# Two products for each block in the even input projection, with both sums added by VectorE

## Chip, cores and metric

The kernel runs on one core of one Trainium2 chip. The metric is the device time of one execution in microseconds; of the kernel before there are three runs, and their median counts.

## The reference, cut to what matters

A trunk of two layers on 256 tokens with 2048 features. The first (even) layer begins with one projection `z`, which feeds a recurrence (part A, 16 heads of 64 features) and a gated linear recurrence (part B).

```
z = x @ ev_w_in                                   # 256 x 2048 times 2048 x 5408
# part A, columns 0 .. 3359: r, k, v and three low-rank pieces
z = z + (token_shift(z) - z) * mu                 # token_shift: one token back
r, k, v, w_lo, a_lo, g_lo = split_cols(z, A_SIZES)
kk = k * k_k;  kk = kk / max(sqrt(sum(kk * kk)), 1e-12)      # by head
...                                               # recurrence over the tokens, group norm, gate
# part B, columns 3360 .. 5407
xb, gate = split(z, 2)
xc = causal_dwconv(xb, conv_w, conv_b)            # 4 taps
...                                               # two gates from xc, a scan over the tokens
y_b = gelu(gate) * h
y = concatenate([y_a, y_b]) @ ev_w_out
```

Then come layer norm, a feed-forward part, a gated addition, and the second (odd) layer, which the change leaves as it is.

## The kernel before, in words

Features lie on the 128 partitions and the 256 tokens in the columns. Each weight and each activation is held as a high and a low part, and a product is the sum of high x high, high x low and low x high. The activations' parts lie side by side in one tile of 512 columns (`hls[k]`: high in columns 0 to 255, low in 256 to 511). `wchunk` (L110) loads half a row of weights (128 x 1024, SP's queue), and ScalarE (`hi`) and VectorE (`lo`) split it, in this layer in slices of 256 columns.

`mm3` (L134) has two forms. With `one`, a block of 128 features takes three matmuls of 256 columns into the first half of a PSUM bank (L138, L139, L140). Without it, the high weights take both parts in one matmul of 512 columns into the whole bank (L142) and the low weights the high part into its first half (L143); the two halves of the bank have then to be added, which `evac` (L186) does: ScalarE copies the second half to SBUF, VectorE adds the first. `gproj` (L145) runs a row of 16 blocks and yields 0.32 us (`BLOCK`) after each; it is a generator, so that a row can be taken piece by piece.

The even layer's input projection has 43 rows of weights (`evin`), all with `one=True`:

- 3 rows for the low-rank pieces (`lora`, L645), one after the other at the start;
- 3 rows for each of 8 pairs of heads (`stage1`, L657; "a head" below is such a pair): block(1) for the keys, block(0), block(2) for the values;
- 2 rows for each of 8 steps of part B (`rglru`, L919): one for the convolution, one for the gate.

`shifted` (L634) takes the rows of part A: ScalarE scales the sum in PSUM by 1 - mu (L638), VectorE adds the sum one token back, scaled by mu (L639). `rglru` reads its first row's PSUM in one ScalarE operation (L924) and three of VectorE (L927), and its second row's in a gelu (L959).

TensorE's order is the program's. `run` (L1027) takes the recurrence of a head (`stage2`, L751), whose steps yield about how long TensorE would wait, and fills each such time with pieces of `filler` (L1012): the next head's `stage1`, then `rglru`, and with the last head the first rows of the output projection. Two places of this order matter below.

- In `stage1`, block(1) is followed by the scaling and shift of `kr`, by `kk` and its square; eight blocks of block(0) are emitted, then the sum of the squares over a head's features (`group_pow`, L293), whose power POOL takes; later the result is spread out (L284).
- In `stage2`, two matmuls (L814) give B, which ScalarE copies; then a loop of 15 steps on VectorE, each a product and a sum, works on its columns and ends in Dt, which TensorE takes at L780. After each step two blocks of the filler are emitted.

ScalarE and VectorE instructions of `stage1` and `stage2` are emitted through `Ahead` (L49 in the profile), which lets them come before others that were emitted up to 20 and 60 instructions earlier; those of `shifted`, `evac` and `rglru` have no such right. All engines run in the order fixed when the program is built. Tiles of the tag `t` come from a ring of 11, PSUM banks of these rows from a ring of 3 (`pp`).

Of the kernel before, what the change touches and what calls it, by code (L numbers as in the profile page):

```python
# [30 lines left out]
def drain(g):  # L31
    """runs a generator to its end and returns what it returns"""
    while True:
        try:
            next(g)
        except StopIteration as e:
            return e.value


class Ahead:  # L40
    """an engine whose instructions come before those emitted up to n instructions earlier, where it has the choice"""
# [11 lines left out]
class Core:  # L53
# [21 lines left out]
    def load_const(self, n, after):  # L75
        """a table of constants, loaded once after is there: the loads that come first are short of bandwidth"""
        t = getattr(self, n)
        self.nc.scalar.copy(t[:, 0:1], after[:, 0:1])
        self.nc.sync.dma_start(t, self.a[n])
# [18 lines left out]
    def xt(self, m, name, dt=F32R, w=2 * S):  # L98
        """a tile for block m of 16, in one of two rings that hold 8 blocks and one more"""
        return self.xpool.tile([P, w], dt, tag="xa" if m < 8 else "xb", name=self.nm(name))  # L100

    def ps(self, tag=None):
        """a PSUM bank; without a tag, from all of them in turn"""
# [5 lines left out]
    # ---- weights: load, then split into the two parts that single-pass products carry  # L109
    def wchunk(self, src, keep=None):  # L110
        """high and low part of a piece of weights; keep: makes a tile that holds them for longer"""
# [16 lines left out]
    def hl_split(self, dst, src):  # L128
        """dst[:, :256] and dst[:, 256:] become the high and low part of src."""
# [4 lines left out]
    def mm3(self, ps, hi, lo, hl, first, last, one=False):  # L134
        """a block's products; they add up over both halves of ps, or, with one, in its first half alone"""
# [9 lines left out]
    def gproj(self, src, hls, group=8, one=False, more=None, parts=None):  # L145
        """src [128, KT*128] in DRAM, hls the KT activation tiles; returns PSUM [128, 512] whose halves add up
        (one: all in the first). more: (high, low, activations) of one further block, last in the sum;
        parts: src's pieces where they are on chip already. Yields the time of TensorE after each block"""
# [14 lines left out]
    def pieces(self, srcs, k0=0, group=8, soon=0):  # L163
        """the k-tiles k0 .. of several rows of weights, split by instructions that others wait for less"""
# [5 lines left out]
    def projs(self, srcs, ws, hls, group=8):  # L170
        """proj of several rows side by side, each activation tile serving all of them as soon as it is there;
        ws: the first pieces of the weights"""
# [13 lines left out]
    def evac(self, ps, out):  # L186
        """out = sum of the halves"""
# [5 lines left out]
    # ---- residual and layer norm, features on the partitions  # L193
# [6 lines left out]
    def ln_pre(self, m, hl):  # L200
        """s = alpha * x for one block of 128 features"""
# [5 lines left out]
    def ln_set(self, m, ps, hl):  # L207
        """s = alpha * x + y"""
# [7 lines left out]
    def ln_more(self, m, ps):  # L216
        """s += y, with y in the first half of ps"""
# [3 lines left out]
    def ln_stat(self, m):  # L221
        """the sums of s and s * s over the features grow; those of the last block stay apart"""
# [15 lines left out]
    def ln_end(self):  # L238
        """mean and 1 / deviation of each token, worked out with the tokens on the partitions"""
# [17 lines left out]
    def ln_apply(self, g, b):  # L257
        """the normed activations as high and low tiles"""
# [18 lines left out]
    def tok_bcast(self, src, w, b, tag=None):  # L277
        """src [token of a tile of 128, n] -> PSUM [n-th block of w partitions.., tokens], each value on its w partitions"""
# [8 lines left out]
    def group_pow(self, sq, w, scale, c, op, aux, tmp):  # L287
        """(scale * sum of sq over groups of w features, op, c) ** -0.5 [token, (half of the tokens, group)]"""
# [11 lines left out]
    def group_rsqrt(self, sq, w, scale, c, op, aux, tmp, tag):  # L300
        """group_pow in PSUM, on the group's partitions"""
# [53 lines left out]
    def ple_proj(self, l, phl, half, pool=None):  # L355
        """p Wp / 2 for eight blocks of 128 features: two to a tile of pool, or out to DRAM"""
# [20 lines left out]
    def ple_back(self, l, pool):  # L377
        """the blocks that ple_proj put into DRAM"""
# [7 lines left out]
    def ple(self, l, pool, emit):  # L386
        """x + sigmoid(x Wg) * (p Wp); emit(m, tile) takes the blocks of the result"""
# [7 lines left out]
        for m in range(KD):  # L395
            # x + (tanh(g / 2) + 1) * (p Wp / 2)
# [17 lines left out]
# ---- layout of the inputs  # L414
# [4 lines left out]
def col(v):  # L419
    """feature vector -> [128, n] with feature n*128 + p at [p, n]"""  # L420
    return v.reshape(-1, 128).T


def buckets():
    """bucket of each relative position 127 .. -255 (REL_BUCKETS 32, REL_MAX_DIST 128)"""
# [36 lines left out]
def odd_consts():  # L462
    """centring over the first 64 rows, twice; one-hot buckets"""
# [6 lines left out]
def tile_w(W):  # L470
    """[K, M] -> [M/128, 128, K]: block m holds, for each row p of each block of K, its 128 columns"""
# [4 lines left out]
def lay_out(I):  # L476
    """the inputs as the kernel reads them: moved, repeated or padded with zeros, never computed with"""
# [25 lines left out]
    # even layer  # L503
# [34 lines left out]
    # odd layer  # L538
# [22 lines left out]
# ---- even layer's mixer  # L561
# [9 lines left out]
# TensorE time to fill in between the steps of a recurrence, in us  # L571
# [7 lines left out]
def q(t, w=64):  # L579
    """[128, 4*w] -> [128, 4, w]"""  # L580
    return t.rearrange("p (c w) -> p c w", w=w)


class Even:
# [49 lines left out]
    def shifted(self, m, j, out, parts=None):  # L634
        """z * (1 - mu) + shift(z) * mu, z = block m of the input projection; j its place in mu"""
        nc, k = self.nc, self.k
        ps = yield from k.gproj(k.a["evin"][m], self.x, one=True, parts=parts)
        nc.scalar.mul(out, ps[:, 0:S], self.omu[:, j:j + 1])  # L638
        nc.vector.scalar_tensor_tensor(out[:, 1:], ps[:, 0:S - 1], k.v("mu", j), out[:, 1:], op0=ALU.mult, op1=ALU.add)  # L639
# [17 lines left out]
    def stage1(self, i):  # L657
        """projections of two heads and everything that goes feature by feature"""
# [10 lines left out]
        # decay and in-context rate  # L669
# [765 lines left out]
```

## Time and profile before

| | us |
|---|---|
| median of three runs | 2447.64 |
| the three runs | 2447.42, 2447.64, 2456.84 |
| span of the profiled execution | 2455.2 |
| the profiled execution's own time | not told apart; of the three runs only that of 2456.84 is longer than the span |

The span runs from the first to the last instruction. The time of an execution holds the span and a little around it. Busy shares are of the span. A row of TensorE's timeline shows a start and a modelled length; matmuls overlap, and so the distance from one start to the next is what one costs, not its length.

### The profile page before, as it was taken

How to read it: one execution, taken by the hardware profiler on the slowest of the kernel's cores; microseconds unless marked ns; L12 is line 12 of the kernel's file. 1: busy time of each engine (PE TensorE's matmuls, PEld its weight loads, DVE VectorE, ACT ScalarE, POOL GpSimd, SP SyncE). 2: the span in 40 equal slices, each digit the busy share in tenths (PEclk: the TensorE clock that was granted, in tenths of full speed). 3: DMA queues.
4: the chain of work that ended last, by engine and by line, in shares of the span. 5: the costliest groups of instructions: out<-in, count | busy, mean ns of one | idle time of the engine just before them, and what ended most of it. 6: DMA issues, size and time to landing. Idle time of an engine off the chain costs nothing.

```text
span 2455.2 us, 40424 instructions
## 1 busy us (share of the span) xinstructions
PE 2423.2 (99%) x15136; PEld 2161.8 (88%) x15136; DVE 1790.2 (73%) x3756; ACT 1386.7 (56%) x2612; POOL 88.0 (4%) x98
## 2 busy tenths in 40 slices
PE   8999999999999999999999999999999999999999
PEld 8999999888888888888888998888888888888888
DVE  7888888887777777655569697787777777555577
ACT  6767776456555555443346567465555555444454
POOL 0000000010000000000010030010000000000010
PEclk9999999999999999999999999999999999999999
DMA  7333333656666666666656654555555565566655
GB/s 241 118 123 121 105 116 114 185 176 201 191 190 189 189 190 189 184 188 188 187 172 199 190 155 130 190 181 188 188 186 184 188 187 184 180 188 189 188 170 174
DMA packets 128484, 429.38 MB, mean 175 GB/s; under 512 B 14096, under 2 KB 21920, under 8 KB 128288
## 3 DMA queue, kind: packets, MB, share of 16 engines
q1 hardware_dynamic: 128288, 426.80, 55.9%
q8 instruction: 119, 1.95, 0.3%
q14 instruction: 77, 0.63, 0.1%
HBM read 422.52 MB, written 4.22 MB: 174 GB/s over the span
## 4 chain that ended last, share of the span: by engine, by line
PE 89%; issue 5%; DVE 3%; ACT 2%; DMA 1%; POOL 0%; POOLq 0%; ACTq 0%; DVEq 0%; SPq 0%
PE a L142 27%; PE pp L142 18%; PE a L143 14%; PE pp L143 9%; PE pp L138 4%; PE pp L139 4%; PE pp L140 4%; PE a L780 2%; DVE lo L49 1%; PE a L138 1%; PE a L139 1%; PE a L140 1%; DMA raw<-evin 1%; PE a L814 0%; ACT hi L49 0%
## 5 line engine op out<-in xcount | busy, mean ns | idle before, releaser
L49 DVE TENSOR_TENSOR lo<-raw,hi 128x1024 fp32r<-128x1024 f32 (+4 forms) x1160 | 1008.9, 884 | 499.9 <-ACT hi L49 495.4
L49 ACT CAST hi<-raw 128x1024 fp32r<-128x1024 f32 (+4 forms) x1160 | 860.7, 768 | 792.0 <-PE a L142 325.4
L142 PE MATMUL a<-x,hi 128*128 128x512 f32 x2048 | 725.4, 397 | 9.0 <-DVE x L273 9.0
L143 PE MATMUL a<-x,lo 128*128 128x256 f32 x2048 | 572.0, 279 | 0.0
L142 PEld LDWEIGHTS a<-x,hi 128*128 128x128 f32 x2048 | 385.3, 188 | 102.9 <-DVE x L273 11.0
L142 PE MATMUL pp<-x,hi 128*128 128x512 f32 x1248 | 445.0, 397 | 3.6 <-DVE x L273 3.6
L143 PEld LDWEIGHTS a<-x,lo 128*128 128x128 f32 x2048 | 386.6, 189 | 0.4 <-DVE lo L49 0.2
L143 PE MATMUL pp<-x,lo 128*128 128x256 f32 x1248 | 348.5, 279 | 0.0
L142 PEld LDWEIGHTS pp<-x,hi 128*128 128x128 f32 x1248 | 234.9, 188 | 62.3 <-DVE x L273 6.3
L142 PE MATMUL a<-g,hi 128*128 128x512 f32 x792 | 277.7, 393 | 0.0
L138 PE MATMUL pp<-x,hi 128*128 128x256 f32 x800 | 248.3, 310 | 6.7 <-ACT x L131 6.7
L143 PEld LDWEIGHTS pp<-x,lo 128*128 128x128 f32 x1248 | 235.6, 189 | 0.1
L139 PE MATMUL pp<-x,hi 128*128 128x256 f32 x800 | 226.1, 283 | 0.7 <-DVE x L132 0.7
L140 PE MATMUL pp<-x,lo 128*128 128x256 f32 x800 | 226.7, 283 | 0.0
L143 PE MATMUL a<-g,lo 128*128 128x256 f32 x792 | 221.0, 279 | 0.0
L142 PE MATMUL pp<-g,hi 128*128 128x512 f32 x528 | 185.3, 393 | 0.0
L142 PEld LDWEIGHTS a<-g,hi 128*128 128x128 f32 x792 | 148.4, 187 | 35.3
L138 PEld LDWEIGHTS pp<-x,hi 128*128 128x128 f32 x800 | 152.4, 191 | 11.1 <-ACT x L131 6.7
L139 PEld LDWEIGHTS pp<-x,hi 128*128 128x128 f32 x800 | 152.7, 191 | 5.4 <-issue 3.6
L321 ACT ACTIVATE cv<-u,vec_sb 128x256 f32<-128x256 f32 x176 | 105.6, 600 | 88.1 <-DVE u L318 85.8
L140 PEld LDWEIGHTS pp<-x,lo 128*128 128x128 f32 x800 | 151.2, 189 | 0.2 <-issue 0.2
L143 PEld LDWEIGHTS a<-g,lo 128*128 128x128 f32 x792 | 148.4, 187 | 0.0
(415 smaller groups left out, 3407.8 us busy)
## 6 DMA issues: line engine op xcount, KB each, us to landing
raw<-up SPq DMA_DIRECT2D x352, 512.0 KB, 4.5
raw<-dn SPq DMA_DIRECT2D x160, 512.0 KB, 3.7
raw<-evin SPq DMA_DIRECT2D x86, 512.0 KB, 4.1
raw<-pg SPq DMA_DIRECT2D x64, 512.0 KB, 4.5
raw<-odout SPq DMA_DIRECT2D x32, 512.0 KB, 4.5
raw<-evout SPq DMA_DIRECT2D x16, 512.0 KB, 3.8
raw<-dn SPq DMA_DIRECT2D x32, 256.0 KB, 2.7
raw<-evout SPq DMA_DIRECT2D x16, 448.0 KB, 3.4
```

Source lines behind the costliest of these rows:

```text
L49: return getattr(self.eng, name)(*args, **kw)
L138: nc.tensor.matmul(ps[:, 0:S], hi, hl[:, 0:S], start=first, stop=False)
L139: nc.tensor.matmul(ps[:, 0:S], hi, hl[:, S:2 * S], start=False, stop=False)
L140: nc.tensor.matmul(ps[:, 0:S], lo, hl[:, 0:S], start=False, stop=last)
L142: nc.tensor.matmul(ps[:, 0:2 * S], hi, hl, start=first, stop=False)
L143: nc.tensor.matmul(ps[:, 0:S], lo, hl[:, 0:S], start=False, stop=last)
L321: nc.scalar.activation(y, u[:, 2:], AF.Identity, bias=self.v(f"cb{l}", j), scale=self.v(f"cw2{l}", j))
L780: T.matmul(ps[:, c * P:(c + 1) * P], lhs[:, c * P:(c + 1) * P], AR4[:, c] if rhs is AR else rhs[:, c * P:(c + 1) * P], start=True, stop=True)
```

## The change

The rows of the even input projection are computed in the second form of `mm3`: `one=True` is dropped from the three calls of `gproj`. Each row's two halves are added by `evac`, in `shifted` and for the convolution into a new tile `z` of the ring `t`, which the operations behind then read in the place of PSUM, and for the gate into `g`, on which the gelu then works in place. The loads, the order of the rows, the fill times and everything else stay. The diff also takes comments out; these parts are left out here.

```
     def shifted(self, m, j, out, parts=None):
         nc, k = self.nc, self.k
-        ps = yield from k.gproj(k.a["evin"][m], self.x, one=True, parts=parts)
-        nc.scalar.mul(out, ps[:, 0:S], self.omu[:, j:j + 1])
-        nc.vector.scalar_tensor_tensor(out[:, 1:], ps[:, 0:S - 1], k.v("mu", j), out[:, 1:], op0=ALU.mult, op1=ALU.add)
+        ps = yield from k.gproj(k.a["evin"][m], self.x, parts=parts)
+        z = k.t("z")
+        k.evac(ps, z)
+        nc.scalar.mul(out, z, self.omu[:, j:j + 1])
+        nc.vector.scalar_tensor_tensor(out[:, 1:], z[:, 0:S - 1], k.v("mu", j), out[:, 1:], op0=ALU.mult, op1=ALU.add)
...
     def rglru(self, j, yout):
-        ps = yield from k.gproj(k.a["evin"][27 + 2 * j], self.x, one=True)
+        ps = yield from k.gproj(k.a["evin"][27 + 2 * j], self.x)
+        z = k.t("z")
+        k.evac(ps, z)
         xc = self.r1("xc")
-        A.activation(xc, ps[:, 0:S], AF.Identity, bias=k.v("bconv_b", j), scale=k.v("bconv3", j))
+        A.activation(xc, z, AF.Identity, bias=k.v("bconv_b", j), scale=k.v("bconv3", j))
         for n in range(3):
             d = 3 - n
-            V.scalar_tensor_tensor(xc[:, d:], ps[:, 0:S - d], k.v(f"bconv{n}", j), xc[:, d:], op0=ALU.mult, op1=ALU.add)
+            V.scalar_tensor_tensor(xc[:, d:], z[:, 0:S - d], k.v(f"bconv{n}", j), xc[:, d:], op0=ALU.mult, op1=ALU.add)
...
-        rest = k.gproj(k.a["evin"][28 + 2 * j], self.x, one=True)
+        rest = k.gproj(k.a["evin"][28 + 2 * j], self.x)
...
         ps = yield from rest
         g = self.r1("g")
-        A.activation(g, ps[:, 0:S], AF.Gelu_apprx_tanh)
+        k.evac(ps, g)
+        A.activation(g, g, AF.Gelu_apprx_tanh)
```

## Rows read from the trace of the kernel before

**Rows 1.** The head of the page: the span, and each engine's busy time, share of the span and instructions.
```profile
span 2455.2 us, 40424 instructions
...
PE 2423.2 (99%) x15136; PEld 2161.8 (88%) x15136; DVE 1790.2 (73%) x3756; ACT 1386.7 (56%) x2612; POOL 88.0 (4%) x98
```

**Rows 2.** The table of stretches: the stretch in us from the span's start and its length, then each engine's busy time with its instructions, the granted clock of TensorE, the busy share of the DMA engines and GB/s. The last stretch lies in the feed-forward part of the even layer.
```profile
0.00:50.00 50.00, 42.26 (x320) 41.17 (x320) 37.58 (x112) 35.26 (x92) 3.59 (x10) 1.00 0.78 268
...
200.00:250.00 50.00, 49.81 (x391) 47.17 (x389) 42.59 (x141) 37.42 (x104) 2.35 (x2) 1.00 0.36 114
...
600.00:700.00 100.00, 100.00 (x578) 87.42 (x578) 72.59 (x127) 57.23 (x90) 0.00 (x0) 1.00 0.62 190
```

**Rows 3.** Waits of TensorE, of the stretches 0 to 50 us and 410 to 460 us: engine, operation and line, what it waited for, us in total, times, the longest.
```profile
PE a L293 <- ACT sq L49: 0.2, 1, 0.2
...
PE a L780 <- DVE Dt L49: 0.9, 1, 0.9
```

**Rows 4.** DMA issues of the whole program, those of the input projection's weights: queue, count, KB each, median us to landing.
```profile
raw<-evin SPq DMA_DIRECT2D x86, 512.0 KB, 4.1
```

**Rows 5.** Timeline of TensorE in two heads: start in us, length in us, engine, line, operation, and what is written and read. L293 of the keys, a block behind another matmul, undisturbed blocks, and the first matmul on Dt.
```profile
113.81 0.53 PE L293 MATMUL a<-cst_sb,sq 128*128 128x32 f32 x4
...
158.59 0.60 PE L835 MATMUL a<-cst_sb,ET 128*128 128x128 f32 x4
158.95 0.36 PE L138 MATMUL pp<-x,hi 128*128 128x256 f32 x1
...
159.38 0.28 PE L138 MATMUL pp<-x,hi 128*128 128x256 f32 x1
...
160.82 0.28 PE L138 MATMUL pp<-x,hi 128*128 128x256 f32 x1
...
162.07 0.53 PE L293 MATMUL a<-cst_sb,sq 128*128 128x32 f32 x4
...
170.36 1.05 PE L780 MATMUL a<-Dt,E 128*128 128x128 f32 x8
```

**Rows 6.** Timeline of TensorE where blocks have two matmuls: rows of the output projection in the last head, and the feed-forward part.
```profile
434.45 0.53 PE L293 MATMUL a<-cst_sb,sq 128*128 128x32 f32 x4
434.81 0.48 PE L142 MATMUL pp<-y,hi 128*128 128x512 f32 x1
...
435.24 0.40 PE L142 MATMUL pp<-y,hi 128*128 128x512 f32 x1
...
440.02 0.40 PE L142 MATMUL pp<-y,hi 128*128 128x512 f32 x1
...
442.85 0.40 PE L142 MATMUL pp<-y,hi 128*128 128x512 f32 x1
...
640.15 0.40 PE L142 MATMUL pp<-x,hi 128*128 128x512 f32 x1
...
642.58 0.39 PE L142 MATMUL a<-x,hi 128*128 128x512 f32 x1
```

**Rows 7.** Prices: first the instructions on the tile ev of `evac` in the whole program (count, ns least, median and most, first and last start), then groups of ScalarE between 110 and 410 us (count, busy us in all, mean ns of one, idle before).
```profile
L190 ACT COPY ev<-pp x78: 347/365/373, 537.8 to 2445.5; 128x256 f32<-128x256 f32 x78
...
L191 DVE TENSOR_TENSOR pl_g<-pp,ev x12: 414/418/424, 1293.1 to 2445.9; 128x256 f32<-128x256 f32 x12
...
L638 ACT ACTIVATE kr<-pp,omu 128x256 f32<-128x256 f32 x6 | 2.9, 475 | 0.1
...
L49 ACT ACTIVATE kk<-kr,vec_sb 128x256 f32<-128x256 f32 x6 | 3.1, 516 | 0.0
```

**Rows 8.** Timeline of ScalarE behind the keys' row in the head at 150 us: the scaling, the copy to E, kk and its square.
```profile
158.82 0.47 ACT L638 ACTIVATE kr<-pp,omu 128x256 f32<-128x256 f32 x1
...
160.10 0.59 ACT L49 COPY E<-a 128x512 f32<-128x512 f32 x1
160.58 0.52 ACT L49 ACTIVATE kk<-kr,vec_sb 128x256 f32<-128x256 f32 x1
...
161.28 0.42 ACT L49 ACTIVATE sq<-kk 128x256 f32<-128x256 f32 x1
```

**Rows 9.** Timeline of ScalarE from the end of the gate's row to the second copy to B, in the same head.
```profile
147.09 1.28 ACT L959 ACT_TABLE_LOAD   x1
148.39 0.38 ACT L959 ACTIVATE g<-pp 128x256 f32<-128x256 f32 x1
148.79 1.28 ACT L952 ACT_TABLE_LOAD   x1
...
150.52 1.28 ACT L49 ACT_TABLE_LOAD   x1
...
155.38 0.59 ACT L49 COPY B<-a 128x512 f32<-128x512 f32 x1
```

**Rows 10.** Timeline of VectorE in the same head: the first product of the column loop, the shift of kr, and Dt. The time in brackets is idle time before the row and what ended it.
```profile
156.04 0.17 DVE L49 TENSOR_TENSOR sub<-B,Mt 128x8 f32<-128x8 f32 x1
...
159.32 0.48 DVE L639 SCALAR_TENSOR_TENSOR kr<-pp,vec_sb,kr 128x255 f32<-128x255 f32 x1 [0.22 <-ACT kr L638]
...
169.28 0.68 DVE L49 TENSOR_TENSOR Dt<-Mt,cst_sb 128x512 f32<-128x512 f32 x1
```

**Rows 11.** Timelines of VectorE and TensorE in the next step of part B: the last tap of the convolution, and the first matmul on its result.
```profile
187.38 0.48 DVE L927 SCALAR_TENSOR_TENSOR xc<-pp,vec_sb,xc 128x255 f32<-128x255 f32 x1
...
190.93 0.59 PE L936 MATMUL a<-xc,bw 128*128 128x256 f32 x2
```

## The prediction

> **What bounds the kernel now.** I read the page's busy times first: TensorE is busy for 99% of the span [rows 1]. That share alone says little, because a matmul's row lasts longer than the distance to the next one. So I went to the table of stretches. The change touches the even layer's input projection alone, which lies in the first 410 us. There TensorE is busy 49.8 of 50 us at a granted clock of 1.00 (its 2.4 GHz level), VectorE 42.6, ScalarE 37.4, and the DMA share is 0.36; in the feed-forward stage VectorE has 36.3 in 50 [rows 2]. So TensorE sets the pace, with VectorE the second, and the first 50 us (DMA share 0.78) are partly a wait for the first loads.
>
> Next the waits of TensorE: the rows of this layer show a handful of short ones, on a ScalarE square in the first head (L293) and on the column loop of the last head (L780, operand Dt) [rows 3]. Between 110 and 410 us the view names none. That doesn't mean room: a wait that is shorter than the tail of the matmul before it is hidden, so I looked at the margins themselves, in the timeline, below.
>
> **What the change saves on TensorE.** There are 43 rows of weights (86 loads of half a row [rows 4]) of 16 blocks, 688 blocks. Three matmuls of 256 columns become one of 512 and one of 256, so 688 matmuls and weight loads go. Price now: four blocks from 159.38 to 160.82 us, 360 ns each; a block behind a matmul of the recurrence takes 430 (158.95 to 159.38) [rows 5]. Price after: the output projection's rows already have the new form in this layer, 8 blocks from 440.02 to 442.85 us, 354 ns each, and 430 behind another matmul (434.81 to 435.24); in the feed-forward stage 7 blocks from 640.15 to 642.58, 347 ns [rows 6]. So an undisturbed block saves 6 to 13 ns and one behind another matmul 0 to 10. About a third of a head's 80 blocks are of the latter kind. I take 8 ns (bounds 4 and 12). The first row waits for its loads and saves nothing: 672 x 8 ns = **5.4 us** (bounds 2.7 and 8.1). The columns streamed are the same 768 in each block, and that is why the gain is this small.
>
> The Trainium skill ("TensorE: Matmul & The Clock Gate", Back-to-back issue gap) speaks against even that: by its spacing of N / 2.4 + 2.5 ns, three of 256 take 327.5 ns and 512 + 256 take 325, an estimate of 2.5 ns a block or 1.7 us in all. The trace has 360 and 347 to 354, so its distances are longer than that rule's; the measured ones are what I use.
>
> **What it adds.** Each row gets a ScalarE copy of the second half and a VectorE add: 365 and 418 ns in the stages that have them [rows 7]. 43 x 0.365 = 15.7 us of ScalarE, 43 x 0.418 = 18.0 us of VectorE. The scaling L638 then reads SBUF: 475 ns becomes about 516, the price of the scaling of kk, which reads SBUF [rows 7]. A head takes 48.26 us (L293 at 113.81 and 162.07 [rows 5]) and has five rows, so VectorE goes from 41 to 43 of 48 us. Neither engine is full, so the work itself lies beside TensorE; I cost it at nothing as work. It covers itself with the weight splits that are done ahead: no wait of TensorE on a split or a load is listed behind 50 us, and if that cover were gone each row would cost its 0.8 us. No DMA is added or moved, SP's queue keeps its order, and POOL only gets its power (behind L293) as much later as L293 is. What costs is **latency in two chains**, since TensorE's order is fixed in the program.
>
> First chain, the normalised keys. Row block(1) ends, then come scaling (L638), shift (L639), kk, its square, and the matmul L293, which stands 8 blocks later on TensorE; everything that TensorE does next is queued behind it. In the head at 150 us the scaling starts at 158.82, kk at 160.58, the square ends at 161.28 + 0.42 = 161.70 [rows 8], and L293 starts at 162.07 [rows 5]. The margin is 0.37 us. The change puts 0.365 + 0.418 + 0.04 = 0.82 us into this chain, plus two handoffs. Bounds: the copy takes the scaling's place, and kk now waits 0.78 us for ScalarE (from the end of the shift, 159.32 + 0.48 [rows 10], behind casts and the copy to E [rows 8]), part of which the longer chain would use up; if all of it is used up, nothing is late; if none is, 0.82 + two handoffs of about 0.33 (the mean of this chain's three gaps) less the margin is 1.2 us late, 8 blocks of saving included. I take the middle, 0.6 us, for seven heads: 4.2. In the first head L293 waits already [rows 3], with nothing to fill in: 0.8. Together **+5.0 us**.
>
> Second chain, the loop over 15 columns on VectorE. It starts with the second copy to B (ScalarE, 155.38 to 155.97 [rows 9]), runs 156.04 to Dt's end at 169.28 + 0.68 = 169.96 [rows 10], and TensorE takes Dt at 170.36 [rows 5]: a margin of 0.40 us. ScalarE's order ahead of B holds the gate row's gelu, which gets a copy ahead of it and a wait for VectorE's add; two rows end inside the loop, and their adds and shifts are queued between its steps (the shift of kr already stops VectorE for 0.22 us [rows 10]). I expect the loop to end about 1.2 us later. TensorE comes later as well (0.6 from L293) and earlier by 28 blocks x 8 ns = 0.2. So 1.2 - 0.6 + 0.2 - 0.4 = 0.4; I take 0.3, because some adds only take the place of a split. Bounds 0 and 1.3. Seven heads: **+2.1 us**. The last head, whose loop TensorE waits for now (0.9 us [rows 3]), has no margin: **+1.5** (0 to 2.4). Once these waits are in, the next late one would be the step L780 on Z.
>
> The RG-LRU chain has room: the last tap ends at 187.86 and L936 starts at 190.93 [rows 11], 3 us for about 1 us more. I cost it at nothing.
>
> **Sum.** -5.4 + 5.0 + 2.1 + 1.5 = +3.2 us. The bounds are -8.1 (all of the gain, no wait) and -2.7 + 19.6 = +16.9 (every wait at its end). The span is 2455.2; of the three runs only the one of 2456.84 can hold it, 9.2 over the median, so the profiled execution would go to about 2460. I put the same difference on the median: 2447.64 + 3.2 = **2450.8 us**. About 0.5%, 12.2 us, is what a measurement of this kernel can tell from no change, so the forecast is no change that can be told; its own range is 2445 to 2456.
>
> **Rivals.**
> (a) The gain stays. The chains are caught by reordering on VectorE and ScalarE, whose splits can give way. For it: the loop's slots are filled with splits; against: margins of 0.37 and 0.40 us beside 0.82 us put in. 2447.64 - 5.4 = 2442.2, down to 2439.5.
> (b) Slower: a fourth table load in each head. Now each head has three in a row (gelu 147.09, then the square root, then back at 150.52, 1.28 us each [rows 9]). The gelu now waits for VectorE's add in the stretch in which VectorE has no gap. If it is put behind the next head's tanh, the tables change once more, B comes 1.28 us later, and the loop with it. The margin of 0.40 is where it decides: 7 x 1.28 = 9.0 on top of +3.2 gives 2459.8. Against: the gate's row ends ahead of that tanh's matmul in the program's order. The Trainium skill ("ScalarE: Activation LUTs", What ACT_TABLE_LOAD costs) puts 1.28 + 1.38 us on every switch; here the gelu starts at 148.39, right behind the load, so the trace has 1.3.
> (c) The change doesn't shorten TensorE: 768 columns take as long in two matmuls as in three, as they do behind another matmul (430 ns in both forms [rows 5, 6]), and the waits come on top: 2447.64 + 8.6 = 2456.2. Against: the undisturbed blocks of 347 to 354 ns [rows 6]. By the Trainium skill's spacing above it would come out close to this, an estimate of -1.7 + 8.6 = +6.9.
>
> **How the numbers follow.** Forecast 0.55, (a) 0.20, (b) 0.15, (c) 0.10. Faster by over 0.5% would need more than the whole gain at its upper bound: 0.02. Slower by over 0.5% is half of (b) and the upper waits, 0.10. The rest, 0.88, is the same. The range 2441 to 2460 leaves out the lowest third of (a), half of (b) and some of the upper waits: under 0.2.
>
> **What would show it.** In the changed profile: 688 fewer matmuls and weight loads; 16-block rows of L142/L143 at 347 to 354 ns a block; ScalarE and VectorE 16 to 18 us busier; L293 of the keys later than its square by the handoff alone, with a TensorE gap of about half a microsecond; Dt's first matmul waiting; a head's period near 48.5 us, from 48.26. I am wrong if the period falls by 0.6 us or more (a), if a head shows four table loads (b), or if blocks still take 358 ns (c).

## The result and the profile after: 1.1% slower

The changed kernel takes 2484.07 us (median of six runs, 2473.09 to 2494.11); the kernel before, run beside it, 2452.80 (2447.42 to 2467.04). The ratio is 1.0113, with a 95% interval of 1.0088 to 1.0139. Forecast were 2450.8 us, a range of 2441 to 2460, and no change that can be told. The medians lie 31 us apart, the fastest executions of the two kernels 25.7. The profiled execution of the changed kernel took 2473.09 us, with a span 16 us longer than that of the kernel before. The later stages run at a pace that differs from execution to execution, whatever the kernel (last section), so the place to look at is the even layer.

**The head of the page, kernel after.** It answers to [rows 1].

```profile
span 2471.3 us, 39140 instructions
...
PE 2420.6 (98%) x14448; PEld 2123.0 (86%) x14448; DVE 1809.4 (73%) x3799; ACT 1407.8 (57%) x2661; POOL 87.0 (4%) x98
```

The 688 matmuls are gone and TensorE is busy for 2.6 us less, but the span is 16 us longer: TensorE now waits. VectorE is busy for 19.2 us more, ScalarE for 21.1. On ScalarE that is less than 43 copies of 0.365 us (15.7) and six further table loads of 1.28 us (7.7, see below) come to, because busy time counts a stretch in which two instructions overlap only once.

**Where the layer ends, before and after.** The first matmul of the output projection (operand y), in the timelines of TensorE of the two kernels: start, length, engine, line, operation.

```profile
406.45 0.39 PE L142 MATMUL pp<-y,hi 128*128 128x512 f32 x1
```

```profile
428.99 0.40 PE L142 MATMUL pp<-y,hi 128*128 128x512 f32 x1
```

So 22.5 us are lost ahead of this point, in the stage that the change touches. This start is the measure of all experiments below: it holds nothing of the later stages.

**The table of stretches, kernel after** (columns as in [rows 2]).

```profile
0.00:50.00 50.00, 38.97 (x192) 33.61 (x193) 34.55 (x104) 33.13 (x86) 3.69 (x10) 0.93 0.75 258
...
200.00:250.00 50.00, 47.06 (x295) 40.53 (x294) 42.33 (x138) 38.32 (x102) 2.14 (x2) 1.00 0.31 109
```

At 200 us TensorE is busy 47.06 of 50 us where it had 49.81 [rows 2]. VectorE is no fuller than before (42.33, before 42.59): no engine has become the bound. The first 50 us have a granted clock of 0.93, which was 1.00.

**Waits of TensorE, kernel after**, in the stretches 0 to 50 and 110 to 430 us (answering to [rows 3]; before there was nothing to list between 110 and 410).

```profile
PE a L293 <- ACT sq L49: 3.5, 1, 3.5
...
PE a L293 <- ACT sq L49: 14.8, 6, 2.5
PE a L782 <- DVE Z L49: 1.1, 5, 0.2
PE a L782 <- ACT Z L49: 1.0, 5, 0.2
```

Most of it is one wait: the sum over the squared keys (L293), 2.5 us in each of six heads and 3.5 in the first. A head takes 51.3 us from one first matmul on Dt to the next; before it was 48.3.

**That wait in the timeline of TensorE, kernel after** (answering to [rows 5]): undisturbed blocks, the last block of the keys' row, the last matmul ahead of L293, L293.

```profile
162.28 0.39 PE L142 MATMUL pp<-x,hi 128*128 128x512 f32 x1
...
162.62 0.39 PE L142 MATMUL pp<-x,hi 128*128 128x512 f32 x1
...
164.47 0.28 PE L143 MATMUL pp<-x,lo 128*128 128x256 f32 x1
...
171.03 0.48 PE L142 MATMUL pp<-x,hi 128*128 128x512 f32 x1
173.95 0.63 PE L293 MATMUL a<-cst_sb,sq 128*128 128x32 f32 x4 [2.44 <-ACT sq L49]
```

The last matmul of the keys' row in the kernel before, in the head at 150 us:

```profile
157.75 0.28 PE L140 MATMUL pp<-x,lo 128*128 128x256 f32 x1
```

An undisturbed block takes 0.35 us; over the layer's heads the median is 350 ns, and it was 358 to 359 before. The saving is there, and it isn't the pace of one execution: the undisturbed blocks of all the runs below take 358 to 362 ns in the old form and 350 to 353 in the new one. But L293 now stands behind the first matmul of the fifteenth block of the next row (counted between 164.47 and 173.95), where the program emits eight blocks, and still waits. From the start of the keys' last matmul to the end of the square it takes 9.4 us (164.47 to 173.49 + 0.41), against 3.95 before (157.75 to 161.70 [rows 8]).

**Why the square is late: ScalarE in the same head, kernel after** (answering to [rows 8, 9]).

```profile
154.07 0.37 ACT L190 COPY ev<-pp 128x256 f32<-128x256 f32 x1
154.46 1.28 ACT L956 ACT_TABLE_LOAD   x1
...
161.94 1.28 ACT L49 ACT_TABLE_LOAD   x1
...
164.58 1.28 ACT L964 ACT_TABLE_LOAD   x1
165.88 0.42 ACT L964 ACTIVATE g<-g 128x256 f32<-128x256 f32 x1
...
167.29 1.28 ACT L49 ACT_TABLE_LOAD   x1
...
170.12 0.38 ACT L190 COPY ev<-pp 128x256 f32<-128x256 f32 x1
...
171.30 0.52 ACT L640 ACTIVATE kr<-z,omu 128x256 f32<-128x256 f32 x1
...
172.78 0.51 ACT L49 ACTIVATE kk<-kr,vec_sb 128x256 f32<-128x256 f32 x1
...
173.49 0.41 ACT L49 ACTIVATE sq<-kk 128x256 f32<-128x256 f32 x1
```

The first line is the copy of the gate's row, at 154.07. The gelu of that row (L964) runs only at 165.88, between two table loads, behind the next head's tanh. Before, the gelu shared its change of tables with the square root, ahead of that tanh: three loads in a row [rows 9]. Now there are four, and two of them stand right in front of the keys' copy, which starts at 170.12 though the keys' last matmul started at 164.47. In the layer the loads go from 24 to 30.

**Why the gelu is late: VectorE in the same head, kernel after.** In brackets is idle time and what ended it.

```profile
157.29 1.29 DVE L49 TENSOR_TENSOR X<-y,cst_sb 128x512 f32<-128x512 f32 x2
158.50 0.68 DVE L49 TENSOR_TENSOR ET<-a,cst_sb 128x512 f32<-128x512 f32 x1
159.10 0.42 DVE L49 TENSOR_TENSOR R<-a,cst_sb 128x256 f32<-128x256 f32 x1
159.43 0.68 DVE L49 TENSOR_TENSOR ak<-a,cst_sb 128x512 f32<-128x512 f32 x1
...
160.79 0.42 DVE L191 TENSOR_TENSOR g<-pp,ev 128x256 f32<-128x256 f32 x1
...
166.33 0.43 DVE L965 TENSOR_TENSOR th<-th,g 128x256 f32<-128x256 f32 x1 [1.22 <-ACT g L964]
```

The add of the gate's two halves starts 6.7 us after its copy. Some 2 us of what VectorE does in between are part B's own steps; most of the rest is the recurrence, among it the operations on X, ET, R and ak, which may come ahead of up to 60 earlier instructions, while `evac` has no such right.

### The profile page after: what moved, and what is told of

Its sections match the earlier page's. It is cut to its first block, busy times and chain, and to the rows that moved or that the text cites. A ratio compares the mean times of both kernels' runs of the same rounds, so it can differ in the third digit from the quotient of the medians.

```text
span 2471.3 us, 39140 instructions
## 1 busy us (share of the span) xinstructions
PE 2420.6 (98%) x14448; PEld 2123.0 (86%) x14448; DVE 1809.4 (73%) x3799; ACT 1407.8 (57%) x2661; POOL 87.0 (4%) x98
## 3 DMA queue, kind: packets, MB, share of 16 engines
q1 hardware_dynamic: 128288, 426.80, 51.9%
## 4 chain that ended last, share of the span: by engine, by line
PE 83%; ACT 7%; issue 5%; DVE 3%; DMA 1%; POOL 0%; SPq 0%; POOLq 0%; ACTq 0%; DVEq 0%
PE a L142 27%; PE pp L142 21%; PE a L143 14%; PE pp L143 10%; ACT hi L49 2%; PE a L782 2%; PE pp L138 1%; PE pp L139 1%; PE pp L140 1%; DVE lo L49 1%; DMA raw<-evin 1%; PE a L138 1%; ACT L49 1%; PE a L139 1%; PE a L140 1%
## 5 line engine op out<-in xcount | busy, mean ns | idle before, releaser
L142 PE MATMUL pp<-x,hi 128*128 128x512 f32 x1936 | 716.1, 407 | 11.8 <-DVE x L132 7.5
L143 PE MATMUL pp<-x,lo 128*128 128x256 f32 x1936 | 547.7, 283 | 0.0
L142 PEld LDWEIGHTS pp<-x,hi 128*128 128x128 f32 x1936 | 367.6, 190 | 96.3 <-DVE x L132 7.5
L143 PEld LDWEIGHTS pp<-x,lo 128*128 128x128 f32 x1936 | 368.4, 190 | 4.6 <-issue 3.8
L143 PE MATMUL pp<-g,lo 128*128 128x256 f32 x528 | 147.3, 279 | 0.0
L322 DVE SCALAR_TENSOR_TENSOR cv<-u,vec_sb,cv 128x256 f32<-128x256 f32 x176 | 84.7, 481 | 55.7 <-ACT cv L321 55.6
L142 PEld LDWEIGHTS pp<-g,hi 128*128 128x128 f32 x528 | 98.9, 187 | 23.6
L143 PEld LDWEIGHTS pp<-g,lo 128*128 128x128 f32 x528 | 98.9, 187 | 0.0
L323 DVE SCALAR_TENSOR_TENSOR cv<-u,vec_sb,cv 128x256 f32<-128x256 f32 x176 | 85.3, 485 | 6.0
L142 PE MATMUL pp<-o,hi 128*128 128x512 f32 x240 | 84.7, 395 | 0.0
```

Source lines behind the costliest of these rows:

```text
L142: nc.tensor.matmul(ps[:, 0:2 * S], hi, hl, start=first, stop=False)
L143: nc.tensor.matmul(ps[:, 0:S], lo, hl[:, 0:S], start=False, stop=last)
L322: nc.vector.scalar_tensor_tensor(y, u[:, 1:1 + S], self.v(f"cw1{l}", j), y, op0=ALU.mult, op1=ALU.add)
L323: nc.vector.scalar_tensor_tensor(y, u[:, 0:S], self.v(f"cw0{l}", j), y, op0=ALU.mult, op1=ALU.add)
```

## The experiments

Three theories were tested. **A**: the gate's late add puts its gelu behind the next head's tanh, and the fourth table load in ScalarE's queue is the cost. **B**: the keys' chain is longer by its own copy and add. **C**: the added work of VectorE and ScalarE costs as such. For the first head alone a fourth was added, **L**: the low-rank rows' own added steps. All kernels were read by the same four numbers from their traces. The loads are those up to 440 us. The period is the mean distance of the first matmuls on Dt from head 3 to head 7. The wait is the time from the start of the matmul ahead of L293 to that of L293, less the 0.12 us that it takes without a wait, as the median of heads 3 to 8; it is up to 0.4 us longer than the gap that the views show, since they count from the modelled end of the matmul ahead.

| kernel | table loads | period, us | wait at L293, us | first y, us | ratio to before, 95% interval |
|---|---|---|---|---|---|
| before | 24 | 48.3 | 0 | 406.5 | |
| after | 30 | 51.3 | 2.8 | 429.0 | 1.0113 (1.0088 to 1.0139) |
| 1 gate_old | 24 | 49.3 | 1.05 | 416.4 | 1.0026 (0.9998 to 1.0055) |
| 2 gate_only | 30 | 51.4 | 1.17 | 425.2 | 1.0082 (1.0052 to 1.0113) |
| 3 keys_old | 30 | 50.9 | 1.03 | 424.2 | 1.0053 (1.0022 to 1.0084) |
| 4 gate_ahead | 24 | 49.1 | 1.12 | 414.4 | 1.0035 (1.0006 to 1.0065) |
| 5 gate_tanh | 17 | 49.0 | 1.22 | 414.3 | 1.0037 (1.0012 to 1.0062) |
| 6 gate_only_tanh | 17 | 48.8 | 0 | 409.3 | 1.0025 (0.9992 to 1.0058) |
| 7 lora_old | 30 | 51.9 | 2.8 | 426.9 | 1.0076 (1.0046 to 1.0106) |
| 8 best1 | 24 | 48.8 | 0 | 408.0 | 1.0018 (0.9989 to 1.0046) |
| 9 load_more | 38 | 50.5 | 1.07 | 419.8 | 1.0069 (1.0039 to 1.0098) |
| 10 all_ahead120 | 24 | 48.9 | 0.55 | 408.7 | 1.0021 (0.9995 to 1.0047) |
| 11 best_conv | 24 | 48.2 | 0 | 406.4 | 1.0002 (0.9975 to 1.0030) |
| 12 before_tanh | 16 | 48.0 | 0 | 404.8 | 1.0001 (0.9971 to 1.0031) |

The intervals of the times are wide against what is asked, so the verdicts rest on the traces.

**1. Gate rows old** (gate_old): the changed kernel, 35 rows new, the gate's eight as before.

```
-        rest = k.gproj(k.a["evin"][28 + 2 * j], self.x)
+        rest = k.gproj(k.a["evin"][28 + 2 * j], self.x, one=True)
...
-        k.evac(ps, g)
-        A.activation(g, g, AF.Gelu_apprx_tanh)
+        A.activation(g, ps[:, 0:S], AF.Gelu_apprx_tanh)
```

> The changed kernel with the gate's row of each step of part B alone taken back to three matmuls and a gelu that reads PSUM; 35 of 43 rows keep the two products. Theory A (order: the gate's add on VectorE comes late, the gelu falls behind the next head's tanh, a fourth table load per head stands in ScalarE's queue ahead of the keys' copy): 3 table loads per head, L293 of the keys waits 0.5 us or less (2.9 in the changed kernel), a head's period (first matmul on Dt to the next one) 47.8 to 48.5 us, time within 0.3% of the kernel before. Theory B (the keys' own chain is longer by a copy and an add, as predicted): L293 still waits 2 to 3 us, period 50.5 to 51.3. Theory C (VectorE and ScalarE simply have more to do): the loss falls with the rows, four fifths of it stay, period about 50.7.

The six loads are gone, a head takes 49.3 us instead of 51.3, and 12.6 of the 22.5 us come back although only 8 of the 43 rows are undone. What is left here, 1.05 us of wait per head, is B's size; the first head keeps 3.9 us of wait. Neither theory has it alone: the period lies between A's 47.8 to 48.5 us and B's 50.5 to 51.3.

**2. Gate rows alone new** (gate_only): the kernel before with 8 rows of 43 in the new form.

```
-        rest = k.gproj(k.a["evin"][28 + 2 * j], self.x, one=True)
+        rest = k.gproj(k.a["evin"][28 + 2 * j], self.x)
...
-        A.activation(g, ps[:, 0:S], AF.Gelu_apprx_tanh)
+        k.evac(ps, g)
+        A.activation(g, g, AF.Gelu_apprx_tanh)
```

> The kernel before with the gate's row alone in two products and evac; the other 35 rows as before. Theory A: 4 table loads per head, L293 waits 1 to 2 us, period 49.3 to 50.5 us (48.2 before, 51.3 in the changed kernel), since the keys' scaling stands in the same queue behind the loads. Theory B: the keys' chain is as before, no new wait, period 48.1 to 48.3. Theory C: a fifth of the loss, period 48.9.

Waits of TensorE between 110 and 400 us in this kernel:

```profile
PE a L293 <- ACT sq L49: 6.0, 6, 1.0
PE a L781 <- DVE Z L49: 5.3, 6, 1.3
PE a L781 <- ACT bd_vb L49: 4.6, 6, 0.8
```

Eight rows, a fifth of the added work, lose 18.7 us of the layer and bring all six loads. The keys' row is old here, so the wait on its square is not B's: 2.56 us of loads stand ahead of its scaling. The same delay reaches two more products, those on Z and on the copies bd_vb. So the period, 51.4 us, lies above the 49.3 to 50.5 that A had expected from the wait on the square alone. C is out as the main cause: with 8 added rows VectorE has less to do than in gate_old with 35, which is 8.8 us ahead.

**3. Keys' rows old** (keys_old): the changed kernel without the two-product form in block(1).

```
-        ps = yield from k.gproj(k.a["evin"][m], self.x, parts=parts)
-        z = k.t("z")
-        k.evac(ps, z)
+        one = m >= 3 and m % 3 == 1
+        ps = yield from k.gproj(k.a["evin"][m], self.x, one=one, parts=parts)
...
```

> The changed kernel with the keys' row of each head (block(1)) alone taken back to three matmuls and a scaling that reads PSUM; all others, the gate's too, in two products. Theory A: 4 table loads per head stay, L293 still waits 1.5 us or more, period 49.5 to 51. Theory B: no wait at L293, period about 48. Theory C: four fifths of the loss, period 50.7.

The wait at L293 falls from 2.8 to 1.03 us (A had expected 1.5 or more), but the period only from 51.3 to 50.9: the products on bd_vb and Z, which were hidden behind that wait, now wait themselves (4.9 and 3.5 us in six heads). The loads delay everything that ScalarE does behind them; taking away one waiter shows the next. So B alone explains little of the loss.

**4. The gate's add and gelu let ahead** (gate_ahead): all 43 rows stay new.

```
-        k.evac(ps, g)
-        A.activation(g, g, AF.Gelu_apprx_tanh)
+        with k.tc.high_priority(60):
+            k.evac(ps, g)
+            A.activation(g, g, AF.Gelu_apprx_tanh)
```

> The changed kernel, all 43 rows in two products, with the gate's evac and gelu emitted with the right to come before what was emitted up to 60 instructions earlier, so that its add isn't put behind the recurrence's instructions on VectorE. Theory A: 3 table loads per head, the wait at L293 falls from 2.9 to under 1 us, period 48.0 to 49.3. Theory B: the keys' chain is as long as in the changed kernel, wait 2 to 3 us, period 50.5 to 51.3. Theory C: no work has gone, period 51.

ScalarE in the head at 150 us of this kernel, and the add on VectorE:

```profile
150.84 0.37 ACT L190 COPY ev<-pp 128x256 f32<-128x256 f32 x1
151.23 1.28 ACT L956 ACT_TABLE_LOAD   x1
...
152.96 1.28 ACT L965 ACT_TABLE_LOAD   x1
154.25 0.42 ACT L965 ACTIVATE g<-g 128x256 f32<-128x256 f32 x1
...
154.93 0.47 ACT L49 ACTIVATE ta<-a,half 128x256 f32<-128x256 f32 x1
```

```profile
151.50 0.42 DVE L191 TENSOR_TENSOR g<-pp,ev 128x256 f32<-128x256 f32 x1
```

The add follows its copy after 0.7 us, the gelu is ahead of the tanh again, 24 loads, and 14.6 of the 22.5 us are back, with every row still in the new form. The wait left at L293, 1.12 us, is just over the expected 1. This is the strongest evidence for A: no row was taken back, only the place of the work changed, and with it six loads went.

**5. Tanh for gelu, all rows new** (gate_tanh). The gate's function is another one here, which needs no change of tables at this place; the add stays where it was.

```
-        A.activation(g, g, AF.Gelu_apprx_tanh)
+        A.activation(g, g, AF.Tanh)
```

> The changed kernel with tanh in place of gelu in the gate row, so a different gate is computed; the row's two sums are still copied and added late, and two of the four table loads of a head go (24 become 14 for the layer's heads, as the program lists them). If the table load that the late gelu brings is what ScalarE's queue loses (theory A1): the first product on the squares waits about 1.0 us per head as with the gate row in its old form, a head takes 49.0 to 49.5 us, the output projection begins at 414 to 417 us. If the late add itself, or VectorE's place in that chain, is the cost (A2): the wait stays 2.5 us or more and a head takes 50.5 to 51.3 us.

The wait at L293 is 1.22 us, a head takes 49.0, the output projection begins at 414.3, as with the gelu let ahead (414.4): the loads, not the late add, as A says. Tanh takes loads out of the kernel before as well, which is worth 1.7 us there (experiment 12), so these do not explain the 14.7. Seventeen loads remain in the layer where fourteen were expected.

**6. Tanh for gelu, gate rows alone new** (gate_only_tanh): the kernel of experiment 2, the gate's function again another one.

```
-        A.activation(g, g, AF.Gelu_apprx_tanh)
+        A.activation(g, g, AF.Tanh)
```

> The kernel before with the gate row alone in the new form and tanh in place of its gelu, so a different gate is computed. A1 (the table load): with no load left to add, a head takes 48.0 to 48.5 us, the product on the squares waits for nothing (1.17 us with gelu), the output projection begins at 403 to 408 us. A2 (the late add itself): a head takes 50 to 51.3 us as with gelu and the output projection begins at 418 us or later.

The only wait of TensorE listed between 110 and 400 us:

```profile
PE a L781 <- DVE Z L49: 0.7, 3, 0.3
```

The wait on the square is gone (1.17 us with gelu), and 15.9 of the 18.7 us that experiment 2 lost; 1.7 of these are what tanh saves in the kernel before too (experiment 12). The period, 48.8 us, and the layer's end, 409.3, lie a little above the expected 48.0 to 48.5 and 403 to 408. Against the kernel before with tanh, which takes 48.0 us a head, about 0.8 us per head are due to the late add and the added work themselves.

**7. Low-rank rows old** (lora_old): the changed kernel with the first three rows in the old form.

```
-        ps = yield from k.gproj(k.a["evin"][m], self.x, parts=parts)
-        z = k.t("z")
-        k.evac(ps, z)
+        one = m < 3
+        ps = yield from k.gproj(k.a["evin"][m], self.x, one=one, parts=parts)
+        if one:
+            z = ps
+        else:
+            z = k.t("z")
+            k.evac(ps, z)
...
```

> The changed kernel with the three low-rank rows that stand ahead of the first head back in their old form. If their added copy and add are what makes the first head late (theory L): its product on the squares waits under 0.5 us instead of 3.7 and the first product of its column loop starts at 73 to 74 us instead of 76.8. If it is something else in the first head: the wait stays above 3 us. Heads 2 to 8 keep 51.3 us each and 2.8 us of wait by either.

Waits of TensorE up to 110 us (those at L293 belong to the first two heads):

```profile
PE a L293 <- ACT sq L49: 0.6, 2, 0.5
```

The first head's product on the squares waits 0.3 us instead of 3.7, and its first matmul on Dt starts at 72.7 us instead of 76.8 (before: 72.9). Theory L holds. The layer ends only 2.1 us earlier: from 230 us on the heads take longer than in the changed kernel, and there the granted clock falls (last section).

**8. Only r, v and the convolution new** (best1): gate, keys and low-rank rows old, 24 rows new; the gate as in experiment 1, and in `shifted` the edit of experiment 7 with

```
+        one = m < 3 or m % 3 == 1
```

> The changed kernel with the gate rows, the keys' rows and the three low-rank rows in their old form; 24 rows (r, v and the convolution's) keep two products per block: 384 blocks at 6 to 9 ns = 2.3 to 3.5 us less of matmuls. By theory A + B (late gelu, keys' chain) nothing of what was lost remains: 24 table loads in the layer, no wait on the squares, a head takes 47.8 to 48.3 us, the output projection begins at 403 to 407 us, and the time is within 0.3% of before. If VectorE's added work by itself costs (theory C), the wait for the products of the column loop stays at about 0.9 us per head and a head takes 48.7 us or more.

Waits of TensorE between 110 and 400 us:

```profile
PE a L284 <- DVE grb L281: 2.5, 6, 0.4
PE a L786 <- ACT Z L49: 1.1, 6, 0.2
```

No wait on the square and no added load, as expected (in gate_old, where the keys' rows are new, that wait is 1.05 us), but the period is 48.8, not 47.8 to 48.3, and the layer ends at 408.0, not by 407: the spread of the keys' norm (L284) now waits for VectorE. Here C has its share: a head is 0.5 us longer although 48 of its blocks are 8 ns shorter (0.4 us), so by this estimate the added steps cost about 0.9 us per head.

**9. More loads, nothing else** (load_more): the kernel before, all rows old; behind the next head's second tanh ScalarE applies a gelu to one column, into a tile that nothing reads.

```
         A.activation(ta, ps[:, 0:S], AF.Tanh, scale=0.5, bias=self.hv(1, i))
+        if i > 0:
+            one = self.R.tile([P, 1], F32, tag="one", name=k.nm("one"), bufs=1)
+            A.activation(one, ta[:, 0:1], AF.Gelu_apprx_tanh)
```

> The kernel before, all rows old, with one addition: behind the next head's second tanh ScalarE applies a gelu to one column into a tile that nothing reads, in seven heads. That adds two table loads per head (24 in the layer become 38) and no work of VectorE or TensorE. By theory A1 (loads in ScalarE's queue ahead of the keys' copy) 2.56 us + 0.2 us come into the queue; less the margin of 0.4 us and the 0.8 us for which the squared keys' factor waits for ScalarE anyway, the product on the squares waits 1.2 to 2.0 us per head, a head takes 49.5 to 51 us and the output projection begins at 415 to 425 us. By theory C (VectorE's added work or the late add is what costs) a head stays at 48.2 to 48.5 us and the output projection begins before 409 us.

ScalarE in the head at 150 us of this kernel, and TensorE's waits between 110 and 400 us:

```profile
155.01 1.28 ACT L49 ACT_TABLE_LOAD   x1
156.31 0.20 ACT L49 ACTIVATE one<-ta 128x1 f32<-128x1 f32 x1
...
159.25 1.28 ACT L49 ACT_TABLE_LOAD   x1
160.54 0.42 ACT L49 ACTIVATE P<-L 128x256 f32<-128x256 f32 x1
```

```profile
PE a L293 <- ACT sq L49: 5.5, 6, 0.9
PE a L783 <- ACT Z L49: 3.8, 6, 0.7
PE a L783 <- DVE Z L49: 1.1, 5, 0.3
```

Two loads and one column of gelu, some 2.8 us of ScalarE per head, cost 2.2 us per head and 13.3 us of the layer with not one row changed, though ScalarE is busy for only 37.8 of 50 us at 200 us in that kernel. The wait at L293 (1.07) lies just under the expected 1.2; the rest falls on Z. This is the cost of loads alone, close to what A needs. The Trainium skill ("ScalarE: Activation LUTs", What ACT_TABLE_LOAD costs) puts 2.66 us on each switch, drain included, an estimate of 5.3 us for these two; here the column starts 0.02 us behind the end of its load, so the trace has 1.3 us for one, half of that.

**10. The added steps of 32 rows let ahead** (all_ahead120): low-rank rows old, the other 40 new; the gate as in experiment 4, the convolution's eight rows without the right, and in `shifted`, for the keys', r's and v's rows:

```
+        with k.tc.high_priority(120):
+            z = k.t("z")
+            k.evac(ps, z)
+            nc.scalar.mul(out, z, self.omu[:, j:j + 1])
+            nc.vector.scalar_tensor_tensor(out[:, 1:], z[:, 0:S - 1], k.v("mu", j), out[:, 1:], op0=ALU.mult, op1=ALU.add)
```

> The changed kernel with the low-rank rows old, the gate's add and gelu let ahead of up to 60 instructions emitted earlier, and the added copy, add, scaling and shift of the keys', r's and v's rows let ahead of up to 120. If place in the queues is all that costs (A + B): 24 table loads, the wait on the squares under 0.4 us, a head takes 47.6 to 48.3 us and the output projection begins at 401 to 406 us, 0 to 5 us ahead of the kernel before. If the added length of the keys' chain can't be hidden (B alone): the wait stays at about 1 us and a head takes 49 us.

Waits of TensorE between 110 and 400 us (L791 is the product on Dt and Z here):

```profile
PE a L791 <- ACT hi L49: 3.0, 6, 0.5
PE a L293 <- ACT sq L49: 2.4, 6, 0.4
```

The wait on the square halves and Dt becomes late instead, by 0.5 us: place is not all. With 40 rows new, the layer ends 2.2 us behind the kernel before, so the 5 us of matmuls are spent on two waits, and neither "place alone" (401 to 406) nor "B alone" (49 us and a wait of 1) is quite right. That Dt's wait has the label of a weight split rather than of Dt's own operation is the profile's inference: in the head at 170 us Dt ends on VectorE at 170.43, and the product starts at 170.57.

**11. Only the convolution new** (best_conv), 8 rows; the gate as in experiment 1, and in `shifted`:

```
-        ps = yield from k.gproj(k.a["evin"][m], self.x, parts=parts)
-        z = k.t("z")
-        k.evac(ps, z)
+        ps = yield from k.gproj(k.a["evin"][m], self.x, one=True, parts=parts)
+        z = ps
...
```

> The changed kernel with only the eight convolution rows in the new form: 128 blocks at 6 to 9 ns = 0.8 to 1.2 us less of matmuls. If the waits left with r's, v's and the convolution's rows new (for the normalised spread, 0.75 us per head, and for the step on Z, 0.5) come from r's and v's adds in VectorE's queue, both go: a head takes 48.0 to 48.3 us and the output projection begins at 405 to 406.5 us. If they come from the convolution's, a head stays near 48.8 us. The time is within 0.3% of before by either.

A head takes 48.2 us, the layer ends at 406.4, the time is that of the kernel before. So the waits of experiment 8 came with r's and v's rows. The saving, expected at 0.8 to 1.2 us, can't be seen.

**12. Tanh for gelu in the kernel before** (before_tanh), again another function.

```
-        A.activation(g, ps[:, 0:S], AF.Gelu_apprx_tanh)
+        A.activation(g, ps[:, 0:S], AF.Tanh)
```

> The kernel before with tanh in place of gelu in the gate row (a different gate): fewer table loads with all rows old. TensorE is the bound there, with no wait, so by A1 fewer loads give nothing: a head stays at 48.2 to 48.4 us and the output projection begins at 404 to 407 us. A head below 47.8 us would mean that the loads cost the kernel before something as well.

A head takes 48.0 us, 0.2 less than with gelu and than expected: of the loads that stand together early in a head, one fewer gives the kernel before almost nothing. Eight loads fewer give 1.7 us of the layer here, while two more at another place cost 2.2 us in each head (experiment 9). The place of a load decides its price.

None of the versions is faster than the kernel before by more than can be told.

## Why the prediction was wrong, step by step

**The saving** was right: 8 ns a block were forecast, and the traces have 358 to 359 and 350 ns in undisturbed blocks. Behind another matmul it is smaller, 441 and 437 ns. Rival (c) is out.

**The added work as such**: 18 us for VectorE and 15.7 for ScalarE were forecast, 19.2 and 21.1 came (the latter with six loads of 1.28 us). "I cost it at nothing as work" was nearly right: experiments 6 and 8 show the exception, 0.5 us per head more than the kernel before in each.

**The failed step** is the treatment of the gate's row, in the second chain and in rival (b). The prediction saw that the gelu would get "a copy ahead of it and a wait for VectorE's add", and priced only the loop behind it. The keys' chain, where the loss came, holds nothing for it in the sum. The prediction did not follow what VectorE has queued ahead of that add, 6.7 us, most of it the recurrence, and took "the gate's row ends ahead of that tanh's matmul in the program's order" as a reason against the fourth load. But the built order is not that of the program's text: the add was passed by instructions that have the right to come ahead, and with that right of its own (experiment 4) it starts 0.7 us behind its copy. Rival (b)'s mechanism came about, in six heads, with a chance of 0.15 given to it, and its own sign, four table loads in a head, is what the trace shows. Its price was wrong as well: it put 1.28 us per head on B and the loop. The runs show 2.2 us per head (periods of 51.3 and 49.1 us, experiment 4; 14.6 of the layer's 22.5 us), on the keys' copy and so on L293, and when that is out of the way on the products on bd_vb and Z. Two loads, not one, stand ahead of the keys' copy.

**"TensorE's order is fixed in the program"** was wrong too. It is fixed when the kernel is built, and the build moved L293 from behind the eighth block of the next row into the fifteenth. The margin of 0.37 us was therefore not the one that decided; but some seven blocks more, 2.3 to 2.5 us, did not cover a chain that grew by 5.5. In gate_old L293 stands in the ninth block, in gate_ahead in the tenth, in gate_only behind the twelfth; in load_more, where the square is late as well, it stays behind the eighth. So what the build goes by is not shown.

**The keys' chain** had the right mechanism, but its price was near the upper bound: 0.6 us per head forecast, at most 1.2; with the added loads gone it waits 1.05 to 1.12 (experiments 1 and 4), although L293 stands one or two blocks further back.

**Dt's loop**: +2.1 and +1.5 us were forecast. Dt itself waits in no head between 110 and 430 us, since TensorE comes later to it; the next in line, Z, named as such, waits 0.4 us. In the last head Dt waits 0.5 us, before 0.9 [rows 3]: the 1.5 did not come either. With place put right (experiment 10) Dt does wait, 0.5 us per head, near the 0.3 forecast.

**The first head**: 0.8 us was forecast, 3.3 more came, from the low-rank rows. They stand one after the other at the very start, and the prediction counted only the keys' row there. Experiment 7 shows that these rows cause it; by which of their steps was not taken apart. Behind that wait the clock took some 2.3 us more (last section), which no term of the prediction holds.

**The upper bound** doesn't add up as written: 7 x 1.2 + 0.8 + 7 x 1.3 + 2.4 are 20.7 us of waits, not 19.6, which would put it at +18.0. The loss in the layer, 22.5 us, lies above either.

The account in the layer: +22.5 us, of which 14.6 are the gelu's place; 5.7 more go when the low-rank rows are old and the keys', r's and v's steps are let ahead (experiment 10); 2.2 remain. These are differences of single executions; how far the layer's end varies from one to the next was not measured, and in lora_old the clock alone seems to have moved it by some 2 us.

## What to carry to other kernels

Where a change puts a step of one engine ahead of an instruction that needs another table, follow that instruction to its new place in its own queue: price the load at what stands behind it there, not by the engine's share of busy time. If a helper's instructions have to feed a chain that others wait for, give them the same right to come ahead as that chain has; here that brought back two thirds of the loss without undoing a row. And where TensorE has no gap, a saving of 2% in its blocks is spent by the first wait that comes with it.

## What the hardware showed besides

**The feed-forward stages run at one of two paces**, chosen anew in each execution and each of the two stages, with a granted clock of 1.00 in both. The stretch from 1700 to 1800 us in the kernel before and in best_conv, the same instructions:

```profile
1700.00:1800.00 100.00, 100.00 (x567) 86.77 (x567) 71.55 (x126) 55.62 (x88) 0.00 (x0) 1.00 0.60 187
```

```profile
1700.00:1800.00 100.00, 100.00 (x579) 87.41 (x578) 72.57 (x127) 57.23 (x90) 0.00 (x0) 1.00 0.58 191
```

567 matmuls against 579 in 100 us, 2.1%, and some 9 us per stage. Of the 14 profiled executions, one takes, less the start of its first y, 2042 to 2044 us with both stages at the quicker pace (gate_old, best_conv, the changed kernel), 2050 to 2054 with one (before, load_more, all_ahead120 and six others), 2059 to 2061 with none (gate_only, gate_tanh). That is most of the scatter of the times: the profiled execution of the changed kernel has both stages quick, that of the kernel before one. Its cause is not known. The 347 ns that the prediction took from the feed-forward part [rows 6] are the quicker pace; at the slower one a block takes 353.

**The granted clock fell behind some of the waits at L293.** The first head of the changed kernel, stretches of 4 us:

```profile
38.00:42.00 4.00, 1.05 (x5) 1.05 (x6) 1.64 (x5) 2.84 (x9) 0.00 (x0) 0.78 0.63 242
42.00:46.00 4.00, 4.00 (x14) 3.42 (x14) 2.20 (x8) 1.22 (x5) 1.12 (x1) 0.50 0.53 185
46.00:50.00 4.00, 4.00 (x23) 3.45 (x22) 3.24 (x12) 2.54 (x8) 0.00 (x0) 0.87 0.21 77
```

TensorE waited 3.5 us at L293; then its granted clock was 0.50, the 1.2 GHz level, and blocks came 0.64 us apart until 47 us, eight of them: 2.3 us lost on top of the wait. In lora_old the same happened behind waits of 2.5 us in heads from 250 us on (0.97 in each 50 us), where the period is 51.9 instead of 51.3; in the changed kernel the same waits left the clock at 1.00 from 150 us on.
